# Five stretches of float32 work in a head in place of eleven, with one of the cached values' loads in the low weights' tile

## The chip, the cores and the metric

The kernel runs on one core of a Trainium2 chip. The metric is the device time of one launch in microseconds, of which the median of several runs is taken. The profile is of one execution.

## The reference

One inference step of a two layer trunk: a group of one prompt of 512 frames, and a sample group of 8 sequences of 16 frames, each with 512 past frames. Layer 0 is a recurrent layer (RG-LRU); then keys and values are made once from the stream, and layer 1 is a stick-breaking attention of 16 heads of 128. The part that the change touches, for the queries `q`, the keys and the values of a head:

```python
def sb_block(q, q_pos, k, v):
    z = jnp.einsum('bqhd,bshd->bhqs', q, k).astype(jnp.float32) * (HEAD_DIM ** -0.5)
    mask = jnp.arange(k.shape[1])[None, :] < q_pos[:, None]
    log_keep = jnp.where(mask, jax.nn.log_sigmoid(-z), 0.0)
    log_after = lax.cumsum(log_keep, axis=3, reverse=True) - log_keep
    attn = jnp.where(mask, jnp.exp(jax.nn.log_sigmoid(z) + log_after), 0.0)
    o = jnp.einsum('bhqs,bshd->bqhd', attn, v.astype(jnp.float32))
    return o.astype(q.dtype)

def stick_breaking_mixer(hn, k_all, v_all, w_in, w_out):
    q, zg = jnp.split(hn @ w_in, 2, axis=-1)
    o = stick_breaking(q.reshape(B, T, N_HEADS, HEAD_DIM), k_all, v_all)
    return (o.reshape(B, T, D_ATT) * jax.nn.silu(zg)) @ w_out
```

For the sample group `k_all` and `v_all` are the 512 cached rows of each sequence followed by the 16 new ones.

## The kernel before

The 640 rows of the two groups are kept transposed, the feature along the partitions. Large products split each float32 operand into a high and a low part in the matmul's rounded float32 and add three matmuls (`mm3`: L108, L109, L110). The layer-1 query product of a head is such a product; it is cut into pieces, and a piece is computed between the steps of the head before, so that TensorE always has matmuls that wait for nothing. In the trace these are the `psh` rows, 320 wide. The transposes and the sample group's own small matmuls are in plain float32.

A head is a list of steps, given as a string in which each letter is a step and `q` a piece of the next head's product. The tile framework's scheduler makes each engine's order from it, by priority in the order of the program, so an engine's order isn't the string's to the letter. The steps:

- P: the prompt's scores, tiles `z3`, `z2`, `z1`, in `mm3` manner (L1702 to L1704), and before the change also the sample group's scores against its new keys `kn` (L1809), 16 small matmuls on the last 32 columns of `z1`'s bank.
- S0, S1: scores of the sample's sequences 0 to 3 and 4 to 7 (g = 0 and 1) against the cached keys `ck`, tile `zc` (L1727). Four sequences are written by four matmuls to 32 rows each of the result (column-tiled: the stationary operand has 32 columns).
- After each score, ScalarE, VectorE and GpSimd make the stick-breaking weights `e3`, `e2`, `e1`, `es0`, `es1` from it.
- V0, V1: transposes of the prompt's weights to the banks `pa` (L1713), copied by ScalarE as high part `ath` (L1719), while VectorE makes the low part `atl` (L1720).
- T0, T1: transposes of the sample's weights, `pas` for the cached rows (L1751), copied to `at`, and `pan` for the new ones (L1755), copied to `an`. Here, too, the two `cv` tiles of cached values for the group are loaded (L1743, 512 KB each, two buffers).
- O: the prompt's output, `po`, by `mm3` from `vh`, `vl`, `ath` and `atl`.
- M0, M1: the sample's output, `pos`, from `an` with the new values `vn` (L1763) and from `at` with `cv` (L1768), column-tiled again.
- C0, C1: ScalarE copies `pos` to `ob`, TensorE transposes it to `pot` (L1775), VectorE multiplies by the gate.
- L, U, N: the loads of the next head's keys `kr` and `kn`, values `vr`, cached keys `ck`. K, W: the split of keys and values in their parts. Z stands in the last head, where the pieces `q` are pieces of the out product `acc` in place of queries.

SyncE issues nearly all loads, in one queue. A load waits in it until the buffer it fills has been read, and holds those behind it. `vr` is loaded into the tile `ath`, which the out matmuls read.

Of the kernel before, what the change touches and what calls it, by code (L numbers as in the profile page):

```python
# [50 lines left out]
class Trunk:  # L51
# [28 lines left out]
    def wsplit(self, src, width):  # L80

        return self.hilo(self.wraw(src, width).rearrange("p a n -> p (a n)"), width)
# [1207 lines left out]
    def attention_consts(self, ap):  # L1290
# [3 lines left out]
        self.mask = [ap.tile([P, n], F32, name=f"mask{i}") for i, n in enumerate((P, TS))]  # L1294
        self.keep = [ap.tile([P, n], F32, name=f"keep{i}") for i, n in enumerate((PAST, PAST + TS))]
# [56 lines left out]
    def query_load(self, h, i):  # L1352
        if h < NHEAD:
            self.qraw[i] = self.wp.tile([P, self.WW], F32, tag=self.raws[i], name="wr", bufs=1)
            self.nc.sync.dma_start(self.qraw[i], self.I["w_in_b"][h, :, 1024 * i : 1024 * i + 1024])
# [84 lines left out]
    def scaled_query(self, j, src, qh, ql, qs):  # L1440
# [6 lines left out]
        if j == 1:  # L1447
            nc.scalar.activation(qs[:, 0:P], src[:, r:], AF.Copy, scale=sc)
            nc.gpsimd.memset(qs[:, P:], 0.0)
# [14 lines left out]
    def query_tiles(self, ap):  # L1464
# [3 lines left out]
        z = ap.tile([P, T], F32, tag="z", name="z", bufs=2)  # L1468
# [37 lines left out]
    def query(self, h, ap):  # L1506
# [36 lines left out]
        def rest(a, c, u2, p5):  # L1543
# [9 lines left out]
            fill("wl", 3)  # L1553
            fill("wh", 3)
# [63 lines left out]
        fill("wh", 2)  # L1618
        yield
        yield from rest(a, c, u2, p5)  # L1620
        product(d, X22)
        evac(zs[1], d, u3, ALU.subtract)
        fill("wh", 3)
# [4 lines left out]
    def sticks(self, ap, parts, width, runs):  # L1628
# [20 lines left out]
        A.activation(e, e, AF.Exp)  # L1649
# [6 lines left out]
    def keys_load(self, h, ap):  # L1656

        dma = self.nc.sync.dma_start
        row = self.O["kT"][P * h : P * h + P, :]
        raw = ap.tile([P, T], F32R, tag="oh", name="kr", bufs=1).bitcast(F32)[:, :TP]  # L1660
        dma(raw, row[:, :TP])
        kn = ap.tile([P, P], F32, tag="kn", name="kn", bufs=1)
        dma(kn, row[:, TP:])
        return raw, kn
# [23 lines left out]
    def attention(self, h, ap, qkv, zs):  # L1688
# [20 lines left out]
        def spread(e, i):  # L1709

            ps = one("pa")
            for j in range(i + 1):
                tr(ps[:, P * j : P * j + P], e[:, P * j : P * j + P], self.ident)  # L1713
            n = min(i + 1, 3)
            src = ps[:, : P * n].rearrange(pd, d=P)
            for sv, hv, lv in [(src, ath[:, :n, P * i : P * i + P], atl[:, :n, P * i : P * i + P])] + (
                [(ps[:, 384:], ath[:, 1, 0:P], atl[:, 1, 0:P])] if i == 3 else []
            ):
                A.activation(hv, sv, AF.Copy)  # L1719
                V.tensor_tensor(lv, sv, hv.bitcast(F32), ALU.subtract)  # L1720


        def sample_scores(g):
# [7 lines left out]
            zn = st["z1"][:, 256 + TS * g : 256 + TS * g + TS]  # L1731
            st[f"es{g}"] = self.sticks(ap, [(zc, 0), (zn, PAST)], PAST + TS, [(0, PAST + TS, 1)])

        def new_values(g):
            t = ap.tile([TS, 4, P], F32, tag="vn", name="vn", bufs=1)
# [5 lines left out]
        def cached_values(b0):  # L1741
            c = ap.tile([P, 8, P], F32, tag="cv", name="cv", bufs=2)
# [3 lines left out]
        def sample_turn(g):  # L1746
            e = st[f"es{g}"]
            st["cv"] = [cached_values(4 * g + 2 * u) for u in range(2)]
# [5 lines left out]
            ps = one("pan")  # L1754
            tr(ps[0:TS, 0:P], e[:, PAST : PAST + TS], self.ident)  # L1755
            an = st["an"] = ap.tile([TS, P], F32, tag="an", name="an", bufs=1)
            V.tensor_copy(an, ps[0:TS, 0:P])

        def sample_out(g):
            at, an, cvs = st["at"], st["an"], st["cv"]  # L1760
            po = one("pos")
            for j in range(4):
                mm(po[32 * j : 32 * j + 32, 0:P], an[:, 32 * j : 32 * j + 32], st["vn"][:, j, :], start=True, stop=False, **kw)  # L1763
            if g == 0:
                st["vn"] = new_values(1)
            for i in range(4):
                for j in range(4):
                    mm(po[32 * j : 32 * j + 32, 0:P], at[:, i, 32 * j : 32 * j + 32], cvs[j // 2][:, 4 * (j % 2) + i, :],  # L1768
                       start=False, stop=i == 3, **kw)
# [3 lines left out]
        def sample_close(g):  # L1773
            ps = one("pot")
            tr(ps[:, 0:P], st["ob"], self.ident)  # L1775
            cs = slice(TP + 64 * g, TP + 64 * g + 64)
# [19 lines left out]
        def prompt_scores():  # L1796
# [7 lines left out]
            z1 = st["z1"] = zt("z1")  # L1804
# [214 lines left out]
```

## Time and profile before

| what | us |
|---|---|
| median of 3 runs (lowest, highest) | 2858.5 (2856.53, 2860.51) |
| span of the profiled execution | 2852.1 |
| up to head 0's first score | 2005.9 |
| head 0, to the first score of head 1 | 45.95 |
| heads 1 to 14 | 550.77 |
| head 15, out product and end | 249.46 |

The profile gives the span from the first to the last instruction; a run's own time includes what lies around it, 6.4 us if the profiled execution stands at the median. Matmul rows of the timeline have the start, the duration, the line, the output and the inputs, and behind that the idle time ahead of them with what released them. A plain float32 matmul shows as two entries in the count (16 matmuls are x32). "128*32" is the stationary tile.

### The profile page before, as it was taken

Reading aid. Unit: us, or ns where it says so; the run is one execution under the profiler, and the core shown is the slowest. Engines: PE = TensorE matmul, PEld = TensorE weight load, DVE = VectorE, ACT = ScalarE, POOL = GpSimd, SP = SyncE. Lnnn points to the kernel's source line nnn. Section 1 sums busy time; section 2 is a strip of 40 time slices with the busy share of each in tenths; the row PEclk is TensorE's granted clock in tenths of the full one; section 3 lists DMA queues with packets and bytes.
Section 4 is the critical chain, followed back from the end, with each engine's and each line's share of the span. In section 5 each row is a group of like instructions: output and inputs, shape, how many; then the busy total and the mean of one; then the engine's idle time right before and its main releaser. Section 6 shows DMA issues by size and latency. Waiting matters only on the chain.

```text
span 2852.1 us, 48054 instructions
## 1 busy us (share of the span) xinstructions
PE 2785.0 (98%) x18340; PEld 2459.3 (86%) x18340; DVE 2034.8 (71%) x3344; ACT 1666.2 (58%) x2846; POOL 439.1 (15%) x732
## 2 busy tenths in 40 slices
PE   6999999999999999999999999999999999999998
PEld 4799999999999987777787899867888889887887
DVE  7678777777777766766866866667877877776335
ACT  5576556655665556665655555553666766666223
POOL 0012212221222111112220000122101111111000
PEclk9999999999999999999999999999999999999999
DMA  9966766676766666676776233575466666668636
GB/s 339 331 145 157 166 161 153 158 164 160 161 149 164 141 228 209 206 251 190 238 255 218 92 117 109 183 267 192 145 205 189 194 197 191 199 199 287 188 111 229
DMA packets 249094, 544.49 MB, mean 191 GB/s; under 512 B 23496, under 2 KB 108616, under 8 KB 247712
## 3 DMA queue, kind: packets, MB, share of 16 engines
q1 hardware_dynamic: 201616, 377.05, 41.2%
q0 software_dynamic: 47248, 164.38, 23.2%
q8 instruction: 144, 2.36, 0.3%
q14 instruction: 86, 0.70, 0.1%
HBM read 499.97 MB, written 41.37 MB: 190 GB/s over the span
## 4 chain that ended last, share of the span: by engine, by line
PE 80%; DVE 4%; ACT 4%; DMA 3%; issue 2%; POOL 0%; SPq 0%; DVEq 0%; POOLq 0%; ACTq 0%
PE acc L108 7%; PE acc L110 7%; PE acc L109 7%; PE pa L108 4%; PE pa L110 4%; PE pa L109 4%; PE psh L108 3%; PE psh L110 3%; PE psh L109 3%; PE pc L110 3%; PE pc L109 3%; PE pc L108 3%; PE acck L108 3%; PE acck L109 2%; PE acck L110 2%
## 5 line engine op out<-in xcount | busy, mean ns | idle before, releaser
L108 PE MATMUL acc<-wh,yh 128*128 128x512 f32 x940 | 371.0, 395 | 0.5 <-ACT wh L93 0.4
L110 PE MATMUL acc<-wh,yl 128*128 128x512 f32 x940 | 365.5, 390 | 1.3 <-DVE yl L962 1.3
L109 PE MATMUL acc<-wl,yh 128*128 128x512 f32 x940 | 366.4, 390 | 0.1
L94 DVE TENSOR_TENSOR wl<-wr,wh 128x1024 fp32r<-128x1024 f32 x151 | 186.5, 1238 | 217.0 <-ACT wh L93 216.6
L93 ACT ACTIVATE wh<-wr 128x1024 fp32r<-128x1024 f32 x151 | 159.6, 1057 | 267.7 <-PE acc L110 220.7
L108 PEld LDWEIGHTS acc<-wh,yh 128*128 128x128 f32 x940 | 176.7, 188 | 54.0 <-issue 15.7
L110 PEld LDWEIGHTS acc<-wh,yl 128*128 128x128 f32 x940 | 176.3, 188 | 38.8 <-DVE yl L962 1.7
L109 PEld LDWEIGHTS acc<-wl,yh 128*128 128x128 f32 x940 | 176.5, 188 | 36.3 <-DVE wl L94 0.7
L193 DVE TENSOR_TENSOR wa<-wa 128x1024 f32<-128x1024 f32 (+1 forms) x160 | 191.5, 1247 | 11.8 <-ACT wa L192 11.2
L110 PE MATMUL pa<-xs,wl 128*128 128x320 f32 x630 | 194.8, 309 | 0.5 <-DVE wl L94 0.5
L108 PE MATMUL pa<-xs,wh 128*128 128x320 f32 x630 | 194.7, 309 | 0.0
L109 PE MATMUL pa<-xs,wh 128*128 128x320 f32 x630 | 194.7, 309 | 0.0
L93 ACT ACTIVATE wh<-sum 128x896 fp32r<-128x896 f32 x102 | 96.9, 950 | 143.0 <-PE pa L109 46.5
L192 ACT ACTIVATE wa<-wa 128x1024 bf16<-128x1024 f32 x160 | 159.3, 1046 | 25.5 <-DVE wa L193 12.0
L546 POOL DMA_DIRECT2D sum<-w_in_a_dram x90 | 79.1, 882 | 490.5 <-DVE wl L94 208.8
L108 PE MATMUL psh<-nh,wl 128*128 128x320 f32 x480 | 150.8, 314 | 2.1 <-DVE z L1535 2.1
L110 PE MATMUL psh<-nh,wl 128*128 128x320 f32 x480 | 150.1, 313 | 0.0
L109 PE MATMUL psh<-nl,wl 128*128 128x320 f32 x480 | 149.4, 311 | 0.0
L93 ACT ACTIVATE wh<-rv 128x256 fp32r<-128x256 f32 (+1 forms) x108 | 51.8, 480 | 145.8 <-PE pa L109 95.2
L108 PE MATMUL acck<-wh,nh 128*128 128x512 f32 x320 | 127.8, 401 | 5.7 <-DVE keep L1263 3.5
L110 PE MATMUL pc<-xs,wl 128*128 128x320 f32 x420 | 129.9, 309 | 0.7 <-DVE wl L94 0.7
L108 PE MATMUL pc<-xs,wh 128*128 128x320 f32 x420 | 130.0, 310 | 0.0
(489 smaller groups left out, 8595.9 us busy)
## 6 DMA issues: line engine op xcount, KB each, us to landing
wa<-w_ada_dram POOLq DMA_DIRECT2D x120, 512.0 KB, 5.2
wr<-w_out_a_dram SPq DMA_DIRECT2D x96, 512.0 KB, 4.5
sum<-w_in_a_dram POOLq DMA_DIRECT2D x90, 448.0 KB, 5.7
wa<-w_ada_dram SPq DMA_DIRECT2D x72, 512.0 KB, 6.4
wr<-w_in_b_dram SPq DMA_DIRECT2D x64, 512.0 KB, 4.3
ck<-cache_k_dram SPq DMA_DIRECT2D x64, 512.0 KB, 5.2
cv<-cache_v_dram SPq DMA_DIRECT2D x64, 512.0 KB, 5.7
wr<-w_out_b_dram SPq DMA_DIRECT2D x55, 512.0 KB, 4.2
```

Of the source, the lines that this page charges most:

```text
L93: self.split_at = nc.scalar.activation(hi[:, :n], raw, AF.Copy).ins
L94: nc.vector.tensor_tensor(lo[:, :n], raw, hi[:, :n].bitcast(F32), ALU.subtract)
L108: mm(out, sh, mh, start=start, stop=False, **kw)
L109: mm(out, sh, ml, start=False, stop=False, **kw)
L110: return mm(out, sl, mh, start=False, stop=stop, **kw)
L192: nc.scalar.activation(parts[i], raw, AF.Copy)
L193: nc.vector.tensor_tensor(parts[2] if i else raw, raw, parts[i], ALU.subtract)
L546: self.nc.gpsimd.dma_start(self.big[tag], self.quarter(w, i), accum_op=ALU.add)
```

## The change

The steps of a head are put in another order: the new keys' scores become a step X with a bank and a small tile `zn` of their own; C1 (as `c1`) is done in the next head, behind X; S1 comes ahead of the weights' transposes, V1 behind T0, and M0 and T1 follow the out matmuls directly. The transposes of the new part of the weights (`an`) move from `pan` into spare columns of V1's bank (`pa`) and of C0's bank (`pot`). M multiplies the cached values ahead of the new ones. The output bank `po` comes from another ring of banks and goes through the blocks from the last to the first, so that the widest matmuls end it.

Of the two cached value tiles of group 1, the first becomes `cva`: it is loaded into the buffer of `atl` as soon as the out matmuls have read that; the new values of group 1 go into the same buffer's third part. The masks become bf16, `kr` and `kn` are loaded as one of 640 columns, `z` has three buffers, and a few instructions are told to be issued after others. The diff, without the masks, imports, initial values and `wsplit`, which is held behind the weights' copies (`turned`):

```diff
-            self.nc.sync.dma_start(self.qraw[i], self.I["w_in_b"][h, :, 1024 * i : 1024 * i + 1024])
+            self.last_load = self.nc.sync.dma_start(self.qraw[i], self.I["w_in_b"][h, :, 1024 * i : 1024 * i + 1024]).ins
...
-            nc.scalar.activation(qs[:, 0:P], src[:, r:], AF.Copy, scale=sc)
+            self.scaled = nc.scalar.activation(qs[:, 0:P], src[:, r:], AF.Copy, scale=sc).ins
...
-        z = ap.tile([P, T], F32, tag="z", name="z", bufs=2)
+        z = ap.tile([P, T], F32, tag="z", name="z", bufs=3)
...
-            fill("wl", 3)
-            fill("wh", 3)
+            with self.tc.issue_after(self.scaled):
+                fill("wl", 3)
+                fill("wh", 3)
...
         u3 = keep(zs[1], a)
-        fill("wh", 2)
         yield
-        yield from rest(a, c, u2, p5)
         product(d, X22)
         evac(zs[1], d, u3, ALU.subtract)
-        fill("wh", 3)
+        yield
+        with self.tc.issue_after(self.weighed):
+            fill("wh", 2)
+        yield from rest(a, c, u2, p5)
         if h < NHEAD - 1:
...
-        A.activation(e, e, AF.Exp)
+        self.weighed = A.activation(e, e, AF.Exp).ins
...
-        dma = self.nc.sync.dma_start
-        row = self.O["kT"][P * h : P * h + P, :]
-        raw = ap.tile([P, T], F32R, tag="oh", name="kr", bufs=1).bitcast(F32)[:, :TP]
-        dma(raw, row[:, :TP])
-        kn = ap.tile([P, P], F32, tag="kn", name="kn", bufs=1)
-        dma(kn, row[:, TP:])
-        return raw, kn
+        raw = ap.tile([P, T], F32R, tag="oh", name="kr", bufs=1).bitcast(F32)
+        with self.tc.issue_after(self.last_load):
+            self.nc.sync.dma_start(raw, self.O["kT"][P * h : P * h + P, :])
+        return raw[:, :TP], raw[:, TP:]
...
-        def spread(e, i):
+        def spread(e, *rows, new=False):
...
-            for j in range(i + 1):
+            n = sum(i + 1 for i in rows)
+            for j in range(n):
...
-            n = min(i + 1, 3)
-            src = ps[:, : P * n].rearrange(pd, d=P)
-            for sv, hv, lv in [(src, ath[:, :n, P * i : P * i + P], atl[:, :n, P * i : P * i + P])] + (
-                [(ps[:, 384:], ath[:, 1, 0:P], atl[:, 1, 0:P])] if i == 3 else []
-            ):
-                A.activation(hv, sv, AF.Copy)
-                V.tensor_tensor(lv, sv, hv.bitcast(F32), ALU.subtract)
...
+            put = new_turn(0, ps) if new else lambda: None
+            parts, c = [], 0
+            for i in rows:
+                m, q = min(i + 1, 3), slice(P * i, P * i + P)
+                parts.append((ps[:, c : c + P * m].rearrange(pd, d=P), ath[:, :m, q], atl[:, :m, q]))
+                if i == 3:
+                    parts.append((ps[:, 384:], ath[:, 1, 0:P], atl[:, 1, 0:P]))
+                c += P * (i + 1)
+            with self.tc.high_priority(200):
+                for sv, hv, lv in parts:
+                    self.turned = A.activation(hv, sv, AF.Copy).ins
+                    V.tensor_tensor(lv, sv, hv.bitcast(F32), ALU.subtract)
+            put()
...
+        def new_turn(g, ps):
...
+            tr(ps[0:TS, 384:], st[f"es{g}"][:, PAST : PAST + TS], self.ident)
+            an = st["an"] = ap.tile([TS, P], F32, tag="an", name="an", bufs=1)
...
+            def put():
+                with self.tc.high_priority(200):
+                    V.tensor_copy(an, ps[0:TS, 384:])
...
+            return put
...
-            zn = st["z1"][:, 256 + TS * g : 256 + TS * g + TS]
+            zn = st["zn"][:, TS * g : TS * g + TS]
...
-        def new_values(g):
-            t = ap.tile([TS, 4, P], F32, tag="vn", name="vn", bufs=1)
+        def new_values(g, t):
...
-        def cached_values(b0):
-            c = ap.tile([P, 8, P], F32, tag="cv", name="cv", bufs=2)
+        def cached_values(b0, c=None):
+            if c is None:
+                c = ap.tile([P, 8, P], F32, tag="cv", name="cv", bufs=2)
...
-            st["cv"] = [cached_values(4 * g + 2 * u) for u in range(2)]
+            st["cv"] = st["early"] + [cached_values(4 * g + 2 * u) for u in range(g, 2)]
...
-            ps = one("pan")
-            tr(ps[0:TS, 0:P], e[:, PAST : PAST + TS], self.ident)
-            an = st["an"] = ap.tile([TS, P], F32, tag="an", name="an", bufs=1)
-            V.tensor_copy(an, ps[0:TS, 0:P])
...
-            at, an, cvs = st["at"], st["an"], st["cv"]
-            po = one("pos")
-            for j in range(4):
-                mm(po[32 * j : 32 * j + 32, 0:P], an[:, 32 * j : 32 * j + 32], st["vn"][:, j, :], start=True, stop=False, **kw)
-            if g == 0:
-                st["vn"] = new_values(1)
+            at, cvs = st["at"], st["cv"]
+            po, an = one("pos"), st["an"]
...
-                       start=False, stop=i == 3, **kw)
+                       start=i == 0, stop=False, **kw)
+            for j in range(4):
+                mm(po[32 * j : 32 * j + 32, 0:P], an[:, 32 * j : 32 * j + 32], st["vn"][g][:, j, :], start=False, stop=True, **kw)
...
+            if g == 0:
+                new_turn(1, ps)()
...
-            z1 = st["z1"] = zt("z1")
+            z1 = zt("z1")
...
+            st["e1"] = self.sticks(ap, [(z1[:, :256], 0)], 256, [(0, 256, 0)])
...
+        def new_scores():
+            ps = one("zn")
...
-                    mm(z1[32 * j : 32 * j + 32, 256 + TS * g : 256 + TS * g + TS], qs[:, q0 : q0 + 32], knT[:, q0 : q0 + TS],
-                       start=False, stop=True, **kw)
-            st["e1"] = self.sticks(ap, [(z1[:, :256], 0)], 256, [(0, 256, 0)])
+                    mm(ps[32 * j : 32 * j + 32, TS * g : TS * g + TS], qs[:, q0 : q0 + 32], knT[:, q0 : q0 + TS],
+                       start=g == 0, stop=True, **kw)
+            zn = st["zn"] = ap.tile([P, 2 * TS], F32, tag="zn", name="zn", bufs=1)
+            A.activation(zn, ps[:, : 2 * TS], AF.Copy)
...
-                spread(st["e2"][:, 384:], 0)
-                spread(st["e1"], 1)
+                spread(st["e1"], 1, new=True)
...
-                spread(st["e2"], 2)
+                spread(st["e2"], 2, 0)
...
-            po = one("po")
-            for i in range(4):
+            po = zt("po")
+            for i in range(3, -1, -1):
...
-                self.mm3(po[:, P * i :], vh[:, i, :], vl[:, i, :], th, tl, i == 0, i == 3)
+                self.mm3(po[:, P * i :], vh[:, i, :], vl[:, i, :], th, tl, i == 3, i == 0, **kw)
...
+            t = ap.tile([P, 3, 512], F32R, tag="atl", name="cva", bufs=1).bitcast(F32)
+            st["early"] = [cached_values(NB // 2, t[:, 0:2, :].rearrange("p a (i d) -> p (a i) d", d=P))]
+            st["vn"].append(new_values(1, t[0:TS, 2, :].rearrange("p (b d) -> p b d", d=P)))
...
-        st = {"vn": new_values(0)}
-        steps = {"P": prompt_scores, "O": prompt_out}
+        st = {"vn": [new_values(0, ap.tile([TS, 4, P], F32, tag="vn", name="vn", bufs=1))], "early": []}
+        steps = {"P": prompt_scores, "X": new_scores, "O": prompt_out}
...
-    LAST = "P S0 q q q S1 V0 q V1 q Z T0 M0 O q C0 q T1 q M1 q C1 q"
-    ORDER = "P q q S0 L q q V0 V1 S1 T0 O U q M0 q T1 N K q C0 M1 W q C1"
+    LAST = "P X c1 S0 q q q S1 V0 q q T0 V1 Z O M0 T1 q q C0 M1 q C1 q"
+    ORDER = "P q q X c1 S0 q q S1 V0 q q T0 V1 L q O U M0 T1 N K q C0 M1 W q"
...
                         steps[step]()
+                    elif step == "c1":
+                        before.get(step.upper(), lambda: None)()
                     elif more and step == "L":
...
                     elif more and step == "K":
-                        k = self.keys_split(ap, keys)
+                        with self.tc.issue_after(self.weighed):
+                            k = self.keys_split(ap, keys)
                     elif more:
-                        v = self.values_split(ap, values)
+                        with self.tc.issue_after(self.scaled):
+                            v = self.values_split(ap, values)
+                before = steps
         return out
```

The next three pairs show what the scheduler makes of that in one of the middle heads; names are as above, `psh` the next head's query product. First TensorE at the end of the out matmuls, before:

```order
L108 MATMUL po<-ath,vh 128x128
L109 MATMUL po<-atl,vh 128x128
L110 MATMUL po<-ath,vl 128x128
L1763 MATMUL pos<-vn,an 32x128 x4
L1768 MATMUL pos<-cv,at 32x128 x16
L110 MATMUL psh<-nh,wl 128x320
L108 MATMUL psh<-nh,wl 128x320
```

After, at the same place:

```order
L112 MATMUL po<-ath,vh 128x512
L113 MATMUL po<-atl,vh 128x512
L114 MATMUL po<-ath,vl 128x512
L1780 MATMUL pos<-cv,at 32x128 x16
L1783 MATMUL pos<-vn,an 32x128 x4
L1771 MATMUL pas<-ident,e 128x128 x4
L112 MATMUL psh<-nh,wl 128x320
```

M0 still follows O, with its cached part first; `pas` of T1, before the change 16 product matmuls later, now stands directly behind it. Second, TensorE at M1, which in both kernels comes 24 product matmuls behind T1. Before:

```order
L110 MATMUL psh<-nh,wl 128x320
L1775 MATMUL pot<-ident,ob 128x128
L1763 MATMUL pos<-vn,an 32x128 x4
L1768 MATMUL pos<-cv,at 32x128 x16
L108 MATMUL psh<-nh,wh 128x320
```

After:

```order
L114 MATMUL psh<-nh,wl 128x320
L1789 MATMUL pot<-ident,ob 128x128
L1734 MATMUL pot<-ident,e 16x128
L1780 MATMUL pos<-cva,at 32x128 x2
L1780 MATMUL pos<-cv,at 32x128 x2
L1780 MATMUL pos<-cva,at 32x128 x2
```

M1 now reads `cva` and `cv` by turns, beginning with `cva`. Third, SyncE's queue, from the second pair of cached keys on. Before:

```order
L1684 DMA ck<-cache_k_dram 128x2x512 x2
L1669 DMA vr<-out_v_dram 128x4x128
L1743 DMA cv<-cache_v_dram 128x8x128 x2
L1355 DMA wr<-w_in_b_dram 128x1024
L1738 DMA vn<-out_v_dram 16x4x128
L1743 DMA cv<-cache_v_dram 128x8x128 x2
L1663 DMA kn<-out_kT_dram 128x128
```

After:

```order
L1687 DMA ck<-cache_k_dram 128x2x512 x2
L1763 DMA cva<-cache_v_dram 128x8x128
L1672 DMA vr<-out_v_dram 128x4x128
L1763 DMA cv<-cache_v_dram 128x8x128
L1757 DMA vn<-out_v_dram 16x4x128
L1763 DMA cv<-cache_v_dram 128x8x128 x2
L1359 DMA wr<-w_in_b_dram 128x1024
```

`cva` now goes ahead of `vr`, and one `cv` of group 1 stays behind it; the pair of the next head follows directly.

More of the change, by code (lines that the diff above doesn't have):

```diff
@@ L1 @@
+from contextlib import ExitStack
 from itertools import chain, cycle, islice
@@ L80, in wsplit @@
     def wsplit(self, src, width):
-        return self.hilo(self.wraw(src, width).rearrange("p a n -> p (a n)"), width)
+        with ExitStack() as ctx:
+            if self.turned is not None:
+                ctx.enter_context(self.tc.issue_after(self.turned))
+            return self.hilo(self.wraw(src, width).rearrange("p a n -> p (a n)"), width)
     def hilo(self, raw, width, negative=False):
@@ L1293, in attention_consts @@
         G = self.nc.gpsimd
-        self.mask = [ap.tile([P, n], F32, name=f"mask{i}") for i, n in enumerate((P, TS))]
-        self.keep = [ap.tile([P, n], F32, name=f"keep{i}") for i, n in enumerate((PAST, PAST + TS))]
+        self.mask = [ap.tile([P, n], BF16, name=f"mask{i}") for i, n in enumerate((P, TS))]
+        self.keep = [ap.tile([P, n], BF16, name=f"keep{i}") for i, n in enumerate((PAST, PAST + TS))]
         for v in self.mask + self.keep:
@@ L1858, in heads @@
             k, v = self.keys_split(ap, keys), self.values_split(ap, values)
+            before = {}
             for h in range(count):
@@ L1890, in run @@
         tc, nc, I, O = self.tc, self.nc, self.I, self.O
-        from contextlib import ExitStack
         with ExitStack() as ctx:
@@ L1895, in run @@
             self.banks = [2, 3, 4, 5, 0, 1]
-            self.local, self.stay = {}, ()
+            self.local, self.stay, self.turned = {}, (), None
             mctx = E(ExitStack())
```

## The prediction

> **What bounds the kernel now.** I read the page's head first, then the stage table over the heads, TensorE's waits stage by stage, and last the timelines of TensorE and of SyncE's queue.
>
> ```profile
> span 2852.1 us, 48054 instructions
> PE 2785.0 (98%) x18340; PEld 2459.3 (86%) x18340; DVE 2034.8 (71%) x3344; ACT 1666.2 (58%) x2846; POOL 439.1 (15%) x732
> ...
> L110 PE MATMUL acc<-wh,yl 128*128 128x512 f32 x940 | 365.5, 390 | 1.3 <-DVE yl L962 1.3
> ```
>
> (The last row is for the length of a 512 wide matmul, 390 ns, used below.)
>
> TensorE is busy 98% of the span, so only its work, its waits and its clock count. The span lies 6.4 us under the median of the runs, 2858.5; I make the sum as a difference and add it to the median. The instruction order on TensorE is the same in both kernels up to the heads, so the difference arises in the sixteen heads and in the start of the out product beside head 15. The stage table has the heads 1 to 14 (first score of head 1 to first score of head 15), head 0, and the stretch of half clock in head 15:
>
> ```profile
> 2051.87:2602.64 550.77, 545.99 (x4755) 487.68 (x4754) 424.56 (x800) 372.47 (x829) 67.05 (x140) 1.00 0.64 197
> ...
> 2005.92:2051.87 45.95, 41.67 (x320) 35.24 (x318) 41.38 (x82) 33.41 (x78) 4.51 (x8) 1.00 0.48 146
> ...
> 2629.90:2636.70 6.80, 4.40 (x37) 3.00 (x38) 1.23 (x1) 2.28 (x3) 0.00 (x0) 0.50 0.93 318
> ```
>
> Columns: length, busy PE, PEld, DVE, ACT, POOL, granted clock, DMA share, GB/s. A head takes 550.77/14 = 39.34 us, and TensorE is without work for 550.77 - 545.99 = 4.78 us in all fourteen, 0.34 a head. That is all that waits can give back there; VectorE (77%) and ScalarE (68%) have room. The waits, first of heads 1 to 14, then of head 15, then of head 0:
>
> ```profile
> PE pa L1713 <- DVE atl L1720: 3.0, 4, 0.9
> PE pan L1755 <- DVE atl L1720: 0.3, 1, 0.3
> PE pot L1775 <- ACT ob L1771: 0.2, 1, 0.2
> ...
> PE pos L1768 <- DMA cv<-cache_v_dram: 5.2, 2, 4.0
> PE pa L1713 <- DVE atl L1720: 0.6, 1, 0.6
> PE acc L108 <- ACT wh L93: 0.4, 1, 0.4
> ...
> PE psh L108 <- DVE z L1535: 2.1, 1, 2.1
> PE zc L1727 <- issue: 1.0, 1, 1.0
> ```
>
> In no head from 1 to 14 does TensorE wait for a transfer. That is the point on which the change turns, since it moves the transfers.
>
> **The change, part by part.**
>
> *Fewer episodes.* Eleven stretches of float32 work per head become five, with the same transposes and the same column-tiled matmuls (`zc`, `pos` and the new keys' scores, which write 32 columns each). What a stretch costs:
>
> ```profile
> 2221.32 0.30 PE L110 MATMUL psh<-ks,wh 128*128 128x320 f32 x1
> 2221.55 1.07 PE L1727 MATMUL zc<-ck,qs 128*32 128x512 f32 x8
> 2222.55 0.41 PE L108 MATMUL psh<-nh,wh 128*128 128x320 f32 x1
> 2222.80 0.31 PE L109 MATMUL psh<-nl,wh 128*128 128x320 f32 x1
> ...
> 2238.62 0.27 PE L110 MATMUL po<-ath,vl 128*128 128x128 f32 x1
> 2238.82 0.42 PE L1763 MATMUL pos<-vn,an 16*32 16x128 f32 x8
> 2239.17 1.08 PE L1768 MATMUL pos<-cv,at 128*32 128x128 f32 x32
> 2240.18 0.41 PE L110 MATMUL psh<-nh,wl 128*128 128x320 f32 x1
> ...
> 2242.49 0.31 PE L110 MATMUL psh<-nh,wl 128*128 128x320 f32 x1
> 2242.64 0.60 PE L1751 MATMUL pas<-ident,e 128*128 128x128 f32 x4
> 2243.07 0.27 PE L1755 MATMUL pan<-ident,e 128*16 128x128 f32 x1
> 2243.10 0.39 PE L108 MATMUL psh<-nh,wl 128*128 128x320 f32 x1
> 2243.33 0.30 PE L109 MATMUL psh<-nl,wl 128*128 128x320 f32 x1
> ...
> 2246.70 0.27 PE L1775 MATMUL pot<-ident,ob 128*128 128x128 f32 x1
> 2246.90 0.42 PE L1763 MATMUL pos<-vn,an 16*32 16x128 f32 x8
> 2247.25 1.08 PE L1768 MATMUL pos<-cv,at 128*32 128x128 f32 x32
> ```
>
> From 2243.33 to 2246.70 stand 23 product matmuls: 0.1465 us each. Four transposes take 2243.07 - 2242.64 = 0.43, so 0.108 each. A transpose stretch then has no price of its own: 2242.49 to 2243.33 is 0.84 us, and two product matmuls and five transposes make 0.29 + 0.54 = 0.83. A column-tiled group has one: `zc` starts 0.23 after the last product matmul (0.085 over its pace), and the second product matmul behind it starts 0.25 after the first (0.10 over). Before, a head has five such groups (new keys, S0, S1, M0, M1), all followed by ordinary float32r work; after, it still has five, and three are followed by transposes instead (new keys by `pot`, S1 by `pa`, M0 by `pas`). So all five entries stay, and three exits change. Each gives between nothing (a transpose pays the same) and 0.10. No row of heads 1 to 14 shows such an exit; I take the middle, 0.05: **-0.15 a head** (0 to -0.3).
>
> *Transposes of the weights.* V0 now makes all eight of two blocks in one stretch behind S1, and V1's two come 24 product matmuls (3.5 us) later instead of after nine. The waits for `atl` were there because VectorE's subtractions hold the banks; they go (-0.29 a head is what I take: the 3.5 us of listed waits are 0.25, all the idle time 0.34). What is late next is the second half of the same chain: V1 and T0 stand in one stretch, and the out matmuls 24 product matmuls behind must find both parts written. That leaves about as much room as before; nearest is the wait that goes, between 0 and 0.9 a head. I take **+0.1**. The rest (weights' parts, key split, `zn` copy, one more `z` buffer, masks in bf16, 320 KB of keys in one load instead of 256 and 64) I cost at nothing: the cover is the third of ScalarE's and the quarter of VectorE's time that is free.
>
> *The values' loads.* This is the large term. Before, the 16 matmuls of M0 free both `cv` buffers, both loads of group 1 start, and M1 comes after 16 product matmuls, T1, and 24 more:
>
> ```profile
> 2238.92 0.37 SPq L1669 DMA_DIRECT2D vr<-out_v_dram  x1
> 2240.28 0.99 SPq L1743 DMA_DIRECT2D cv<-cache_v_dram  x2
> ...
> vr<-out_v_dram SPq DMA_DIRECT2D x1, 256.0 KB, 2.7
> ...
> cv<-cache_v_dram SPq DMA_DIRECT2D x1, 512.0 KB, 4.6
> ...
> cv<-cache_v_dram SPq DMA_DIRECT2D x1, 512.0 KB, 5.8
> ...
> cv<-cache_v_dram SPq DMA_DIRECT2D x56, 512.0 KB, 5.7
> ```
>
> (The last row is the median over heads 1 to 14; the two above it are the pair of the second row, which issue at 2240.28 and, within its 0.99, at 2240.70.) The pair lands at 2244.9 and 2246.5; M1 reads it at 2247.25. So 0.75 us are to spare, and the second half MB lands 1.6 us behind the first. After, T1 is joined to M0, so 16 product matmuls (2.34 us) no longer stand in this window; to make up for it one of the two loads, `cva`, starts when the out matmuls have read `atl`. Count from the start of the last out matmul, t = 0. It is 512 wide now, so M0 enters at 0.32 (0.20 in the row for 128 wide, and 0.12 for the longer matmul, by the durations 0.39 and 0.27 of such shapes). M0's cached part is 2240.18 - 2239.17 = 1.01, its new part 0.35, `pas` 0.48, 24 product matmuls 3.52, two transposes 0.22, entry 0.09: M1 starts at 6.0 and needs the second load after two more instructions, about 6.05. The queue: `cva` at 0.1 (`vr` above went out 0.30 behind the matmul that released it, and the reader of `atl` is one matmul earlier), `vr` behind it at 0.6, and `cv`, which still waits for M0's cached part, at 0.32 + 1.01 + 0.1 = 1.4. It is the third in a queue of 1.25 MB. The pair of 1 MB took 2246.5 - 2240.28 = 6.2 us from first issue to last landing; 256 KB more at 1.6 us per 512 KB are 0.8: 0.1 + 6.2 + 0.8 = 7.1. TensorE waits 7.1 - 6.05, **+1.05 a head**. The ends: if `cv` lands 4.6 after its own issue, as a first of a pair, that is 6.0, no wait; if it takes the 5.8 of a second and 0.8 for `vr`, 8.0, a wait of 2.0. I take 1.05, since the whole queue is what the pair's row measures. Behind the waiting M1 stand the next head's scores, so nothing else fills it; SyncE's next loads are early by a whole head.
>
> [...]
>
> Sum for heads 1 to 14: 14 x (1.05 + 0.1 - 0.29 - 0.15) = 14 x 0.71 = **+9.9 us**.
>
> *Head 15 and the out product.*
>
> ```profile
> 2626.42 0.27 PE L110 MATMUL po<-ath,vl 128*128 128x128 f32 x1
> 2630.73 0.64 PE L1768 MATMUL pos<-cv,at 128*32 128x128 f32 x4 [4.04 <-DMA cv<-cache_v_dram]
> 2632.50 1.92 PE L1768 MATMUL pos<-cv,at 128*32 128x128 f32 x28 [1.12 <-DMA cv<-cache_v_dram]
> ...
> 2622.77 1.96 SPq L1743 DMA_DIRECT2D cv<-cache_v_dram  x2
> ```
>
> Its first pair of `cv` is issued at 2622.77, behind a queue of loads for the out product, and TensorE waits 5.2 us. In the new queue fifteen of these loads and one of weights stand between the last `ck` and that pair, instead of twenty; I take the pair 2.9 us earlier: wait 2.3, -2.9. The only wait of several us is followed by the only half clock in this part: 4.40 us of work at 0.50 (row above), 2.2 us lost. With waits of 2.3 I take the clock as full, -2.2. Against that, M1 of head 15 now comes only 2.2 us behind M0 in place of some 12, and its second load is again issued behind M0: 4.6 less 2.2, +2.4; the evacuation of `ob` has no cover, +0.5; the 0.6 and 0.4 of the other waits I let go by half, -0.5, and the rest at -0.4: **-3.1 us** (-7 to +2).
>
> [...]
>
> *Head 0* is 6.6 us longer than the others, with 3.1 us of the listed waits for VectorE's backlog and a late issue; the new order has the same backlog, **-0.5** (-2.5 to +2).
>
> Total: 9.9 - 3.1 - 0.5 = +6.3, so 2858.5 + 6.3 = **2865**.
>
> **The rivals.**
>
> *The loads stay hidden (the other sign).* `cva` leaves 1.3 us earlier than any load did before, and if the queue serves `cv` within 4.6 us of its issue there is no wait at M1. For it speaks the 4.6 of the first of the pair, against it that a load with another ahead of it took 5.8. It decides from a landing at 6.05. Then 14 x (0.1 - 0.29 - 0.15) = -4.8, with the others -8.4: **2850**.
>
> *VectorE's chain takes the place.* The eight transposes of V0 in one go fill two banks, and if T0 or the out matmuls wait for `atl` in every head as the four did (0.9), this adds 0.8 a head to my sum: 6.3 + 11.2 = +17.5, **2876**. Against it: VectorE is at 77%, and only four of fourteen heads had such a wait.
>
> *The episodes don't count.* That is in my sum: the column-tiled groups stay five. If exits gave their full 0.10 it is -2 us more: 2863.
>
> **How the numbers follow.** A chance of 0.57 that M1 waits 0.6 to 1.6 a head (2859 to 2873), 0.22 for hidden loads (2845 to 2855), 0.13 for VectorE's chain, 0.08 for something between or in head 0 and the tail. A measurement of this kernel tells 0.2%, 5.7 us. The first case is slower by more in 0.33 and the same in 0.20, since its centre lies just beyond that bound; hidden loads are faster in 0.18; VectorE's chain is slower. Together faster 0.26, same 0.28, slower 0.46. The range, 2848 to 2876, leaves out half of VectorE's case and the lower part of the hidden one.
>
> **What would show it.** TensorE's waits in heads 1 to 14 should have a new row, `pos` waiting for a load of `cv` some 14 times, 15 us in all, longest under 2; the waits of `pa` for `atl` should shrink. The `cv` behind `vr` should land 5.5 to 5.9 us after its issue. The head's period should be 40.0. In head 15 the wait at M0 should be about 2.3 and the granted clock 1.00. I am wrong if `cv` lands before M1 in most heads, if `pa` or `po` wait for `atl` in every head, or if the head shortens by far more than 0.4 us without a wait, which would mean that the exits or the stretches cost more than these rows say.

## The result: slower, 2884.6 us against 2859.0, and the profile after

The changed kernel takes 2884.64 us (median of six runs, 2882.91 to 2892.21), the kernel before 2859.03 in the same comparison: +25.6 us, a ratio of 1.0095 with a 95% interval of 1.0084 to 1.0107, so slower by just under 1%. The profiled execution is the one of 2892.2 us, the slowest of the six, with a granted clock of 0.991 on the mean where the others have 0.991 to 0.994; so its sums come out some 8 us larger than the median. A run's own time is 1.7 us longer than its span here (2892.2 and 2890.5). If that holds for the kernel before too, its profiled execution, with a span of 2852.1, took 2853.8 us, some 5 us less than its median; the 6.4 us given above for what lies around the span are then mostly this. For both reasons the two profiled executions differ by 38.4 us where the medians differ by 25.6.

The head of the page first, then the stage table of the profiled execution for heads 1 to 14 and for head 15 with the end (columns as before: length, busy PE, PEld, DVE, ACT, POOL, granted clock, DMA share, GB/s):

```profile
span 2890.5 us, 48087 instructions
PE 2799.2 (97%) x18340; PEld 2468.2 (85%) x18340; DVE 2035.1 (70%) x3344; ACT 1670.3 (58%) x2862; POOL 432.9 (15%) x732
```

```profile
2050.43:2638.01 587.58, 560.42 (x4775) 498.98 (x4773) 429.29 (x809) 378.54 (x845) 60.45 (x140) 0.97 0.60 191
2638.01:2890.50 252.49, 235.43 (x1123) 189.26 (x1119) 109.71 (x144) 86.01 (x135) 12.01 (x21) 0.98 0.61 190
```

Nearly all of it lies in heads 1 to 14: 587.58 us against 550.77, +36.8. Two things are in it. Time without work for TensorE rose from 4.78 to 587.58 - 560.42 = 27.16 us. And the busy time rose from 545.99 to 560.42, mostly because the clock is 0.97 on the mean. A small part is work that moved: head 0's M1, some 1.4 us, now comes 1.5 us behind head 1's first score and so stands in this stretch. Head 1 begins 1.4 us earlier, at 2050.43 in place of 2051.87, so what lies ahead is about as long as it was. The waits of heads 1 to 14:

```profile
PE pos L1780 <- DMA cv<-cache_v_dram: 24.8, 15, 2.3
PE pos L1780 <- DMA cva<-cache_v_dram: 2.3, 1, 2.3
PE pot L1789 <- ACT ob L1785: 0.2, 1, 0.2
```

The waits for `atl` are gone, and M1 waits for the second load of cached values in every head, 1.7 us on the mean (fifteen waits, since head 0's M1 is among them). TensorE's timeline at head 5's M1 shows what follows:

```profile
2255.34 0.41 PE L1780 MATMUL pos<-cva,at 128*32 128x128 f32 x4
2257.95 0.30 PE L1780 MATMUL pos<-cv,at 128*32 128x128 f32 x2 [2.19 <-DMA cv<-cache_v_dram]
...
2259.22 0.65 PE L1783 MATMUL pos<-cva,an 16*32 16x128 f32 x8
2259.80 0.80 PE L1705 MATMUL z<-kh,qh 128*128 128x512 f32 x1
2260.40 0.63 PE L1706 MATMUL z<-kl,qh 128*128 128x512 f32 x1
```

The new values' part, 0.42 us in the timeline before, takes 0.65, and a 512 wide score 0.80 in place of 0.48 to 0.50: the half clock has set in right behind the wait. The clock's record in the trace changes only at steps of 3.41 us on one grid. Here the whole wait lies in one such window, in which TensorE is busy for 1.22 us, and the next window runs at half clock (columns of the stage table):

```profile
2255.18:2258.59 3.41, 1.22 (x31) 0.79 (x30) 2.88 (x7) 2.12 (x5) 0.00 (x0) 1.00 0.85 201
2258.59:2262.01 3.42, 3.42 (x26) 2.35 (x19) 1.47 (x3) 1.26 (x3) 0.00 (x0) 0.50 0.45 129
```

SyncE's queue in the same head:

```profile
2249.52 0.37 SPq L1763 DMA_DIRECT2D cva<-cache_v_dram  x1
2249.98 0.53 SPq L1672 DMA_DIRECT2D vr<-out_v_dram  x1
2250.76 0.37 SPq L1763 DMA_DIRECT2D cv<-cache_v_dram  x1
```

The last out matmul started at 2249.32, so the three go out at 0.2, 0.65 and 1.44. `cv` lands at 8.58.

The fourteen heads fall into two kinds. In some of them a packet of 16 KB of instructions is fetched while `cv` is under way; it holds one DMA engine for 0.98 to 1.32 us. The DMA view from `cva`'s issue to the end of the wait, in head 5:

```profile
q8 instruction: 1, 0.02, 1.0%
issues: line engine op xcount, KB each, median us to landing
cv<-cache_v_dram SPq DMA_DIRECT2D x2, 512.0 KB, 7.1
```

and in head 7, where no row of that queue stands between these:

```profile
q0 software_dynamic: 32, 0.03, 1.3%
issues: line engine op xcount, KB each, median us to landing
cv<-cache_v_dram SPq DMA_DIRECT2D x2, 512.0 KB, 6.0
```

Head 5 has the row of the instruction queue, head 7 hasn't, and there `cv` lands 1.2 us earlier, at 7.38 instead of 8.58. (The rows of `cv` above are medians of this load and the next head's first.) From the packets and the landings of heads 1 to 13 (times from the last out matmul's start; the step is from one `pos` matmul to the next, 0.13 without a wait):

| heads | instruction fetch in the window | `cv` lands | step at M1 | half clock behind it |
|---|---|---|---|---|
| 2, 5, 8, 9, 11, 12 | yes, 0.98 to 1.32 us | 8.38 to 8.58 | 2.27 to 2.46 | in all six |
| 1, 3, 4, 6, 7, 10, 13 | no | 7.38 to 7.83 | 1.26 to 1.72 | behind head 1 alone |

Head 14 has a further reason. Its queue, and on TensorE the two waits behind it:

```profile
2620.10 0.65 SPq L953 DMA_DIRECT2D yl<-odl  x1
2621.38 0.32 SPq L953 DMA_DIRECT2D yh<-odh  x1
2622.84 0.32 SPq L953 DMA_DIRECT2D yl<-odl  x1
2624.66 0.38 SPq L1763 DMA_DIRECT2D cva<-cache_v_dram  x1
```

```profile
2632.82 0.41 PE L1780 MATMUL pos<-cva,at 128*32 128x128 f32 x4 [2.27 <-DMA cva<-cache_v_dram]
2635.57 0.43 PE L1780 MATMUL pos<-cv,at 128*32 128x128 f32 x2 [2.34 <-DMA cv<-cache_v_dram]
```

Seven loads for the out product, 320 KB each, now stand ahead of `cva`; it lands 8.2 us behind the start of the last out matmul, where the other heads have 4.1 to 4.8 (head 8: 5.6). The head takes 44.57 us instead of 39.14.

### The profile page after: what moved, and what is told of

Same layout as the page of the kernel before. It is cut to its first block, busy times and chain, and to the rows that moved or that the text cites. A ratio compares the mean times of both kernels' runs of the same rounds, so it can differ in the third digit from the quotient of the medians.

```text
span 2890.5 us, 48087 instructions
## 1 busy us (share of the span) xinstructions
PE 2799.2 (97%) x18340; PEld 2468.2 (85%) x18340; DVE 2035.1 (70%) x3344; ACT 1670.3 (58%) x2862; POOL 432.9 (15%) x732
## 4 chain that ended last, share of the span: by engine, by line
PE 81%; DMA 5%; DVE 3%; ACT 2%; issue 2%; POOL 0%; DVEq 0%; POOLq 0%; SPq 0%; ACTq 0%
PE acc L112 7%; PE acc L114 6%; PE acc L113 6%; PE pa L112 4%; PE pa L114 4%; PE pa L113 4%; PE psh L112 4%; PE psh L114 4%; PE psh L113 4%; DMA cv<-cache_v_dram 4%; PE pc L114 3%; PE pc L112 3%; PE pc L113 3%; PE acck L112 2%; PE acck L113 2%; PE acck L114 2%
```

## The experiments

The theory from here on: T1 joined to M0 takes 2.35 us from the time in which the second load may land; the load lands late, most of all with an instruction fetch; the longest of these waits bring half clock. The rival: the new stretches, banks and the early load cost the time themselves. Ratios are to the kernel before, run beside each experiment; "heads" are heads 1 to 14 of the profiled execution (550.8 before, 587.6 after).

**The window alone, in the kernel before.**

```diff
-    ORDER = "P q q S0 L q q V0 V1 S1 T0 O U q M0 q T1 N K q C0 M1 W q C1"
+    ORDER = "P q q S0 L q q V0 V1 S1 T0 O U q q M0 T1 N K q C0 M1 W q C1"
```

> The kernel before with one edit: the piece of query product between M0 and T1 goes ahead of M0, so T1 stands directly behind M0 and the window from M0 to M1 loses 2.35 us; all else (eleven stretches, both values' loads behind M0, bank use) stays. The window theory (the loss is the second load landing after M1, and the half clock that follows long waits): the pair lands 6.2 us behind its first issue and is needed at about 4.8, so 1.2 to 1.5 us of wait in heads without an instruction fetch in the window and 2.2 to 2.5 in heads with one, several half clock windows, +25 us or more over before: 2880 to 2895. The rival (the loss comes from the other parts of the change: new stretches, banks, the early load into the weights' tile) expects 2855 to 2865.

2873.66 us, 1.0063 (1.0047 to 1.0078), heads 567.4. Its waits in the heads:

```profile
PE pos L1768 <- DMA cv<-cache_v_dram: 4.2, 10, 0.8
PE pan L1755 <- ACT ob L1771: 2.5, 4, 1.1
PE pa L1713 <- DVE atl L1720: 1.7, 2, 0.9
```

Well over the rival's 2855 to 2865, but less than the theory's number, and the waits are smaller than it said: the new values' part stands ahead of the cached one here, two product matmuls were scheduled between the loads' first uses, and there was one half clock window of 3.4 us. Joining T1 makes the kernel before slower by itself; by the waits listed it is not only the loads that do so, `pan` waits for C0's copy too. Counted from the start of one matmul to the start of the next, 11.4 of the 16.6 us stand ahead of `pos` matmuls and 4.2 ahead of `pan`. The list has less of it, because it counts from the modelled end of the matmul before; also, M1 is now broken in two and TensorE enters it twice. What each of these costs was not tested.

**Without the early load.**

```diff
-            st["cv"] = st["early"] + [cached_values(4 * g + 2 * u) for u in range(g, 2)]
+            st["cv"] = [cached_values(4 * g + 2 * u) for u in range(2)]
...
-            st["early"] = [cached_values(NB // 2, t[:, 0:2, :].rearrange("p a (i d) -> p (a i) d", d=P))]
+            st["early"] = []
```

> The changed kernel without the early load: both cached values' loads of group 1 go into the two cv buffers when M0 has read them, as in the kernel before. Window theory: vr is then ahead by 1.1 us, the pair goes out at 1.44 and 1.9 behind the last out matmul and lands 6.2 after its first issue, 7.6 against 7.4 to 7.9 now, so the early load has brought next to nothing: 2878 to 2892. The rival that the early load, the sharing of the weights' tile or the place of vr in the queue costs the time expects 2860 to 2872.

2878.59 us, 1.0069 (1.0049 to 1.0089), heads 576.2. As the window theory said: the early load brings nothing. The second load of the pair lands at 7.48 to 7.83 in five of the six heads without a fetch, as `cv` does with the early load. It is even faster than the changed kernel, and the two intervals only touch: in the heads with a fetch mostly two waits of 0.5 to 0.8, one for each load, stand where one of 2.0 to 2.2 stood, and the half clock windows that begin in the heads came to 17 us instead of 37.5. The row of its waits (the longest is head 14's):

```profile
PE pos L1780 <- DMA cv<-cache_v_dram: 19.2, 22, 4.7
```

**`vr` behind `cv`.**

```diff
-    ... V1 L q O U M0 T1 N K q C0 M1 W q"
+    ... V1 L q O M0 T1 U N K q C0 M1 W q"
```

> The changed kernel with the step U put behind T1, so that the prompt's values vr (256 KB) are loaded behind the second values' load cv instead of ahead of it; TensorE's order is the same. Queue theory: cv is second in the queue and lands 0.8 us earlier, waits of 0.4 to 0.6 in clean heads and 1.3 to 1.6 in heads with an instruction fetch, few or no half clocks: 2862 to 2870. If cv's landing is set by its own issue and not by what is ahead of it, or if the order and not the wait costs the time, no change: 2880 to 2890.

2865.94 us, 1.0033 (1.0020 to 1.0046): in the middle of what was expected, 18 us below the changed kernel, by the place of one load of 256 KB. But the landing moved by less than the 0.8 I had from the stream: 7.13 instead of 7.53 (medians of the heads without a fetch), 7.74 instead of 8.47 with. The two kinds of heads overlap here: 6.93 to 7.60 without a fetch, 7.50 to 8.14 with one. The stage row of its heads, and their waits:

```profile
2055.84:2620.92 565.08, 546.74 (x4774) 488.00 (x4772) 427.68 (x809) 378.84 (x845) 60.08 (x140) 1.00 0.62 198
```

```profile
PE pos L1780 <- DMA cv<-cache_v_dram: 16.6, 15, 1.7
PE pos L1780 <- DMA cva<-cache_v_dram: 1.6, 2, 1.1
```

The waits fell by a third, from 27.1 to 18.2 us, and the half clock windows from 37.5 to 6.8: no wait is over 1.7 us now, and no half clock is left in heads 1 to 13. Of the 22.5 us between the two stage rows (587.58 and 565.08), 13.7 are busy time, 560.42 to 546.74.

**The wait filled with useless work.** Twelve matmuls of the product's shape ahead of T1's transposes, whose bank they write first:

```diff
             ps = one("pas")
+            for _ in range(12 if g else 0):
+                mm(ps[:, :320], qh[:, 0:P], qh[:, 0:320], start=True, stop=True, **kw)
```

> The changed kernel with 12 useless matmuls of the query product's shape (128x320, rounded float32) ahead of T1's transposes in every head, written to the bank that the transposes then overwrite: 1.76 us more work for TensorE in each head, in the place of the wait. Window theory with half clock caused by the waits: waits shrink to 0 to 0.6, the half clock windows of the heads go, so with more work the kernel is faster than the changed one: 2868 to 2878. If the half clock comes from the lumps of float32 work and not from the wait, its windows stay and the time is 2882 to 2892; if the wait isn't bound to the loads but to something that moves along, 2905 or more.

2881.51 us, 1.0088 (1.0073 to 1.0104), heads 576.0, stage row and waits:

```profile
2052.63:2628.62 575.99, 568.13 (x4940) 511.55 (x4940) 427.59 (x807) 374.32 (x845) 59.69 (x140) 1.00 0.61 194
```

```profile
PE pos L1782 <- DMA cv<-cache_v_dram: 6.7, 7, 2.5
PE pos L1782 <- DMA cva<-cache_v_dram: 1.2, 1, 1.2
```

With 25 us more work in fourteen heads, the heads are 11.6 us shorter in the profiled executions, the waits fall to 7.9 and half clock to one window of 3.4, behind head 14's wait. The float32 stretches are as long as before. So the half clock comes from the waits and not from the stretches. The time itself missed what was expected: the median is outside 2868 to 2878, 3 us below the changed kernel's, and the two intervals overlap. In part that is because the changed kernel's profiled execution has more of the half clock than its median (a granted clock of 0.991, against 0.993 and 0.994 in the two runs around the median).

The longest wait of this list, 2.5 us, is that of head 0's M1, and no half clock followed it. It falls into two windows of the grid, with TensorE busy for 2.29 and 2.09 us:

```profile
2053.79:2057.21 3.42, 2.29 (x15) 1.98 (x15) 0.00 (x0) 0.97 (x2) 0.00 (x0) 1.00 1.15 302
2057.21:2060.62 3.41, 2.09 (x41) 1.69 (x42) 2.18 (x3) 3.17 (x8) 0.00 (x0) 1.00 0.25 62
2060.62:2064.03 3.41, 3.41 (x25) 3.41 (x24) 3.38 (x6) 3.15 (x8) 0.57 (x1) 1.00 0.55 154
```

**A wider window.** One piece of the product from ahead of X to behind T1, 48 matmuls instead of 24 between T1 and M1:

```diff
-    ORDER = "P q q X c1 S0 q q S1 V0 q q T0 V1 L q O U M0 T1 N K q C0 M1 W q"
+    ORDER = "P q X c1 S0 q q S1 V0 q q T0 V1 L q O U M0 T1 N K q q C0 M1 W q"
```

> The changed kernel with one piece of the query product moved from ahead of X to behind T1, so 48 product matmuls stand between T1 and M1 instead of 24 (3.5 us more); V1 then has 12 product matmuls ahead of O instead of 24, and V0 36 ahead of T0. Stretches, banks, early load and queue stay. Window theory: cv lands at 7.4 to 8.6 behind the last out matmul and is needed at 9.5, so no wait at M1 in heads 2 to 13, no half clock there, heads of 38.7 to 39.1 us, the whole 2850 to 2860, where head 14 and the end still lose some us to the out product's loads ahead in the queue. The rival that the new order loses time in itself (VectorE's chain, banks) expects heads over 39.6 and 2868 or more.

2853.20 us, 0.9984 (0.9975 to 0.9993): 0.16% faster than before, and 31 us faster than the changed kernel by one letter's place. All middle heads take 38.93 to 38.97 us; stage row and waits:

```profile
2053.69:2598.70 545.01, 539.05 (x4737) 483.78 (x4733) 421.39 (x803) 376.23 (x844) 54.40 (x140) 1.00 0.66 200
```

```profile
PE zc L1747 <- DVE e L1654: 5.9, 13, 0.5
```

No wait for a load, no half clock, and one new wait, S0 for its bank. The new order, its banks and the early load cost no more in themselves than this wait, 5.9 us in fourteen heads; the rival falls.

**A wider window without the early load** (both edits above).

> The kernel of the wider window, and in it also no early load: both loads of group 1 go into the cv buffers behind M0. Window theory: the pair lands at 7.5 to 8.6 and is needed at 9.5, so no difference to the wider window with the early load, within 4 us, or a little faster in head 14: 2846 to 2858. If the early load has a use, this is slower by 8 us or more.

2852.90 us, 0.9975 (0.9964 to 0.9986). The same as with it: with the window, the tile shared with the weights has no use.

**The out product's loads behind head 14's values** (the wider window, `vr` behind `cv`, and the loads `yh` and `yl` told to follow head 14's last `cv`).

```diff
+                        if getattr(self, "cv_last", None) is not None:
+                            ctx.enter_context(self.tc.issue_after(self.cv_last))
                         nc.sync.dma_start(y.bitcast(F32), part[P * kk : P * kk + P, :])
```

> The kernel of the wider window, with vr behind cv, and with the loads for the out product held until the last values' load of head 14 has been issued. Queue theory for the end: in the changed kernel four pairs of these loads (320 KB each) stand ahead of cva of head 14 and make its M1 wait 2.5 us twice and the clock fall; with them behind it, head 14 takes 39 to 39.6 us instead of 42.5 to 44.6, and the whole is 2 to 5 us below the wider window: 2845 to 2855. Rival: these loads then come late for the out product itself, and the end gets longer by as much: no difference to the wider window.

2856.99 us, 0.9991 (0.9982 to 1.0000). Head 14 takes 38.94 instead of 39.11, so with the wider window it had little left to win, and head 15 with the end takes 251.2 instead of 249.5. The gain that was expected isn't there, as the rival said. Its reason isn't shown: no listed wait at the end names the loads that were held back; those that grew are `pos` for head 15's `cv` (3.0 us instead of 1.3) and `acc` for `wh` (1.7 instead of 0.2). The run also changes two things at once, which it can't tell apart.

**The piece taken from elsewhere**, from between V0 and T0 instead of ahead of X (and no early load).

```diff
-    ORDER = "P q q X c1 S0 q q S1 V0 q q T0 V1 L q O U M0 T1 N K q C0 M1 W q"
+    ORDER = "P q q X c1 S0 q q S1 V0 q T0 V1 L q O U M0 T1 N K q q C0 M1 W q"
```

> The changed kernel without the early load, and with one piece of the query product moved from between V0 and T0 to behind T1 (the wider window took it from ahead of X): again 48 product matmuls between T1 and M1, 60 ahead of X as in the changed kernel, but only 9 product matmuls between V1 and O and 13 between V0 and T0. In the wider window S0 waits 0.45 a head for VectorE to free a bank (5.9 us in all); that wait should go. If V1's copies need no more than the 1.3 us that are left to them, heads of 38.5 and 2843 to 2852; if O has to wait for ath and atl, which the 24 product matmuls of the changed kernel hid, a new wait of 0.3 to 0.9 a head at po takes its place and it is 2850 to 2860. The window theory itself expects no wait for cv in either case.

2854.27 us, 0.9984 (0.9974 to 0.9995). The wait of S0 went, and another took its place, though not the one at `po` that I named: T1's transposes wait for the exponentials of the sample's weights. Heads of 39.00.

```profile
PE pas L1771 <- ACT e L1655: 2.9, 13, 0.4
PE pos L1780 <- DMA cv<-cache_v_dram: 0.7, 1, 0.7
PE zc L1747 <- DMA ck<-cache_k_dram: 0.4, 1, 0.4
```

## Why the prediction was right and wrong, point by point

The sign and the mechanism were right: a new row in the waits, `pos` for `cv`, in every head. The size was not: +6.3 us were forecast and +25.6 measured. The step that failed is the price of that wait. The working took the clock as full behind waits of 2.3 us and had no term for the clock in heads 1 to 14; the runs show up to 17 us of half clock there. It also had one landing time for all heads, where nearly half of them have one about a microsecond later.

*The load's landing, +1.05 a head: in the heads without a fetch nearly right.* The issues came to within 0.1 us of the count, the need at 6.05 too. The landing was 7.1 by the sum and 7.53 in the median of those heads; the wait as listed was 1.2 on the mean. The queue's sum took the pair's length from its first issue. The runs show that the start of the first load hardly counts: `cv` lands 5.7 us behind its own issue as the second in the queue and 6.1 as the third, much as the second of a pair does (5.8); I had named 5.5 to 5.9 for the third. The early first load landed earlier by itself here, at 4.1 to 4.8 in all heads but 8 and 14, and the second didn't follow: 7.38 to 7.83 in the heads without a fetch, and 7.48 to 7.83 in five of the six without the early load.

*Left out: the instruction fetch.* Six of thirteen heads had one, and there the wait is 0.9 us longer. Nothing in my working asked what else uses the DMA engines in a window of 6 us. Before the change the time to spare hid such a landing: the latest one, 8.62 us behind the start of the last out matmul in a head with a fetch, still met M1's cached part at 8.63. That the fetch is the cause is likely, but no run moved it by itself.

*Left out: the half clock behind waits of 2 us.* This is the step that failed most. In the working the clock was bound to the wait of 4.04, and waits of 2.3 in head 15 were taken to leave it alone; in the heads I didn't ask at all, since 1.05 seemed far away. Heads 1 to 14 of the changed kernel hold 34.7 us of windows at clock 0.5, which by estimate cost at most 17.3 us, half their length (a 384 wide score has a step of 0.32 in head 5's and of 0.17 at full clock in head 7). Compared with the wider window, whose heads run at full clock, they have 560.42 - 539.05 = 21.4 us more busy time; the rest is head 0's M1 (1.4) and, by estimate, the modelled ends of the matmuls ahead of sixteen waits, which count as busy (up to 0.28 each: head 5's row above has 0.41, where a step without a wait is 0.13). The -2.2 booked for head 15 took waits of 2.3 us to leave the clock alone; that was my estimate, and no run shows it. A wait of 2.19 us, quoted above, was enough here, and so were the 2.27 and 2.34 of head 14, which leave TensorE 3.00 us without work in one window of the grid. Such a window is 3.41 us long in the trace, but it needn't be idle from end to end: in head 5's TensorE was busy for 1.22 us. The last section has the counts.

*Stretches and order, -0.15 a head: too small.* Without the listed waits a head took (550.77 - 3.5)/14 = 39.09 us before and (545.01 - 5.9)/14 = 38.51 with the wider window, 0.58 less. The exits I had bounded gave little. S1 with V0 in the wider window:

```profile
2264.64 1.07 PE L1747 MATMUL zc<-ck,qs 128*32 128x512 f32 x8
2265.64 1.09 PE L1717 MATMUL pa<-ident,e 128*128 128x128 f32 x8
2266.49 0.39 PE L112 MATMUL psh<-nh,wl 128*128 128x320 f32 x1
2266.72 0.30 PE L113 MATMUL psh<-nl,wl 128*128 128x320 f32 x1
```

The eight transposes and the next product matmul take 2266.72 - 2265.64 = 1.08, and 8 x 0.108 + 0.147 are 1.01: an exit into transposes costs 0.07 where one into a product matmul cost 0.10. M0 with T1's four transposes gives the same 0.07 (2277.74 to 2278.39). The most came from somewhere else. Before, `pan` and the first out matmul stood behind a product matmul with gaps that the list of waits doesn't show:

```profile
2235.93 0.30 PE L108 MATMUL psh<-nh,wl 128*128 128x320 f32 x1
2236.38 0.27 PE L1755 MATMUL pan<-ident,e 128*16 128x128 f32 x1
2236.41 0.39 PE L109 MATMUL psh<-nl,wl 128*128 128x320 f32 x1
2236.77 0.50 PE L108 MATMUL po<-ath,vh 128*128 128x512 f32 x1
```

0.45 and 0.36 us where a step is 0.147, in the mean of seven middle heads 0.39 and 0.36. They are 0.45 a head, and in the new order the step ahead of `po` is 0.150. I had taken the list as complete.

*Transposes of the weights, +0.1 for a new wait and -0.29 for the old ones: nearly right.* No wait for `atl` or `ath` is left in heads 1 to 14, so the old ones went and the new one is 0.

*Head 15, -3.1: wrong.* It is +3.1, 252.49 against 249.41. The wait at M0 went altogether and the half clock there with it, but the rest took more. Counted from matmul start to matmul start, `pos` takes 4.4 us less, `acc` 3.9 more, `po` 2.5 more and the scores `z`, which begin at head 14's half clock, 1.0 more. By the list of waits the out product waits for `wl`, the low part of its weights, which no `acc` did in this stretch before, and `po` waits for `ath`:

```profile
PE acc L113 <- DVE wl L98: 2.7, 4, 0.8
PE po L112 <- ACT ath L1728: 1.6, 1, 1.6
```

And the same move of the queue that I booked as a gain for head 15 put seven loads ahead of head 14's `cva`, which I didn't book at all.

*Head 0, -0.5: can't be told.* Head 1 begins 1.4 us earlier, and head 0's M1 of 1.4 us now comes behind that point.

*Sum.* Heads 1 to 14 of the profiled execution, from before to after: +22.4 us without work (12.0 forecast, 1.05 + 0.1 - 0.29 in fourteen heads), +21.4 more busy time than in the wider window, at most 17.3 of it half clock (0 forecast), and -6.9 from the kernel before to the wider window (-2.1 forecast). The medians lie some 13 us closer together, for the two reasons given with the result; how that splits over these terms no run shows.

The rival of the hidden loads fell, as the pair's row had said: `cv` landed at 7.4 to 8.6 in heads 1 to 13, behind the 6.05 that decides, and 5.9 to 7.1 us after its own issue, where the rival had 4.6. The rival of VectorE's chain fell too.

## What to carry to other kernels

Before a filler is moved out from between a load's issue and its use, write down when the load lands from its own issue in the slowest case, with what else may use the DMA engines, and keep that window; starting one of two loads earlier didn't help the other here. Price a wait in a dense matmul loop with the half clock that may come with it: here a wait of 2.19 us was followed by a window of 3.41 us at clock 0.5, by estimate up to 1.7 us (half its length), nearly as much as the wait. And measure short gaps step to step, since a list of waits leaves some out: the new order was worth 0.58 us a head, most of it such gaps, once 3.5 us of other work had been put back into the window.

## What the hardware showed that was not expected

- In the ten traces the half clock went with how long TensorE was idle within one window of the 3.41 us grid, and not with the length of a wait alone. From 20 us ahead of head 0 to 60 us into head 15, all 22 windows at full clock with more than 1.8 us idle (by the profile's busy times; nine of the 22 in the kernels before and after) were followed by one at half clock, and none of the 1915 with less than 1.37 us; of the 20 between, 10 were. So one wait of 1.4 us in the list was followed by it (head 1 of the changed kernel) and one of the same length wasn't (head 13), two waits of 0.8 and 0.6 in one window were (head 5 of the kernel before with T1 joined), and 2.5 us over two windows weren't (head 0 with the wait filled).
- In the changed kernel, an instruction fetch of 16 KB, about 1.1 us on one of the DMA engines, goes with a 512 KB load that lands 0.9 us later: 8.47 against 7.53 in the median, with no overlap between the two kinds of heads (8.38 to 8.58 and 7.38 to 7.83). This was seen and not made: no run moved the fetch by itself. With the wider window the medians are again 0.9 us apart, but one fetch, late in the load, delayed nothing (7.31).
- The second load in the queue landed 5.8 us behind its own issue without the early load, and 5.7 us with `vr` behind `cv` (medians of the heads without a fetch), where the first had gone out 0.46 and 1.25 us ahead of it.
